# Seven-product quads: T2 subtracted from the weights by an accumulating transfer instead of by VectorE

## The chip, the cores and the metric

The kernel runs on one core of a Trainium2 chip. The metric is the time of one execution on the device in microseconds. Before the change it is 1385.69 us, the median of three runs (1385.48 to 1386.45).

The core has five engines that matter here: TensorE (PE, matrix products into PSUM), VectorE (DVE) and ScalarE (ACT) for elementwise work, GpSimd (POOL), and SyncE (SP), which here only issues transfers (DMAs). Each engine takes its instructions strictly in the order of its own queue and waits at semaphores for the others. Sixteen DMA engines move data between HBM and SBUF.

## The reference

One layer of a hybrid block on x of 256 rows and 2048 columns, in float32: RMS norm, one large projection, a dilated attention branch, a state-space (SSD) branch, gates, and an output projection.

```python
hn = rms_norm(x, norm_w)
proj = hn @ w_in
q, k, v, z_a, z_s, xbc, dt_raw, g_a, g_s = jnp.split(proj, split_points, axis=-1)
# attention of q, k, v in three dilations -> o_a ; scan of xbc, dt_raw -> y
merged = jax.nn.sigmoid(g_a) * (o_a @ w_attn_branch) + jax.nn.sigmoid(g_s) * (y @ w_ssm_branch)
x = x + merged @ w_out
return rms_norm(x, final_norm_w)
```

## The kernel before

All large products are made on TensorE from float32 values split in two: for a weight tile w, ScalarE writes h, a rounded copy, and VectorE writes l = w - h. A product then takes three matmuls (x_h by h, x_h by l, x_l by h; lines 476 to 478, the helper `triple`). The weights (nearly all of the 314.87 MB that are read) are streamed from HBM in units of 128 x 1024 (512 KB) through a ring of five slots (`W_BUFS`), by SP's queue.

Ten wide products use pairs of column blocks and are made by `gemm_pair`: ssm, v, ga, attn and out, each for c = 0 and c = 2. `gemm_pair` goes over the inner dimension in steps of two tiles of 128, called quads, in an order given by a table. A plain quad needs two weight units and 24 matmuls. A quad listed in `S_QUADS` (43 of them) is a Strassen-like step on 2 x 2 blocks: seven products in place of eight, 21 matmuls. Its weight operands are

- `wa`, the unit with the blocks B11 and B21 (loaded, line 522), split into `ha`, `la`;
- `wc`, the block B22 (128 x 512, line 526), split into `hc`, `lc`;
- `wt`, with T1 = B12 - B11 in its left half and T2 = B22 - T1 in its right half, mostly made earlier, kept in HBM (`presum`) and loaded (line 525); for some quads it is made here from a tile `wb` (lines 548 and 555); split into `ht`, `lt` (htt and ltt in the profile);
- `wa` minus T2 on both halves, written over `wa` after `ha` and `la` have read it (line 557), split into `hu`, `lu` (htu and ltu). In part of v, ht, lt, hu and lu lie in a tile `tl_v`.

The helper `part` makes each split: line 543 on ScalarE, line 544 on VectorE; `unit` does it for plain units (lines 276 and 277). Outside v, the tiles of ht and hu have two buffers for both together, so ht of a quad reuses the buffer of the quad before it.

A scheduler in the tile framework sets the order on each engine. The block from line 547 on stands under `tc.high_priority(L_AHEAD)`, which lets a quad's preparation be issued well ahead of its products. GpSimd has little to do in the quads: one-element copies (line 432) on which SP's fetches of the left operands wait.

Of the kernel before, what the change touches and what calls it, by code (L numbers as in the profile page):

```python
# [11 lines left out]
AF = mybir.ActivationFunctionType  # L12
ALU = mybir.AluOpType
PSUM = bass.MemoryType.PSUM

P = 128
# [180 lines left out]
def hybrid_block(ctx: ExitStack, tc: tile.TileContext, wall, xt, x, pk_d, cst_d, fw_d, out):  # L197
    nc = tc.nc
    ve, ac, gp, pe = nc.vector, nc.scalar, nc.gpsimd, nc.tensor
# [24 lines left out]
    def bank(tag, bufs, name):  # L224
        return ps.tile([P, 512], F32, name=name, tag=tag, bufs=bufs)
# [9 lines left out]
    def ring(name):  # L235
        return stream.tile([P, UNIT], F32, name=name, tag="w", bufs=W_BUFS)
# [30 lines left out]
    def unit(n, shape):  # L267
        if n not in loaded:
            load(n)
        w = loaded.pop(n)  # L270
        h = stream.tile([P, UNIT], F32R, name=f"h{n}", tag="h", bufs=H_BUFS)
        l = stream.tile([P, UNIT], F32R, name=f"l{n}", tag="l", bufs=H_BUFS)
        cuts = (0, UNIT // 2, UNIT) if n < N_FINE else (0, UNIT)
        with tc.high_priority(L_AHEAD) if n >= KT // UB else nullcontext():
            for a, b in zip(cuts, cuts[1:]):
                ac.activation(h[:, a:b], w[:, a:b], AF.Copy)  # L276
                ve.tensor_tensor(l[:, a:b], w[:, a:b], h[:, a:b].bitcast(F32), ALU.subtract)  # L277
        for f in on_unit.pop(n, ()):
            f(h[:, 0:1].bitcast(F32))
        k, m = shape  # L280
        return h.rearrange("p (k m) -> p k m", k=k), l.rearrange("p (k m) -> p k m", k=k)
# [34 lines left out]
    def tick(final=False):  # L316
        now[0] += 1
        run_due(float("inf") if final else now[0])
# [142 lines left out]
    def gemm_pair(tag, x_of, n_kt, sxs, swap, extra={}, close=1, order=None, room={}, tail=None):  # L461

        name = f"{tag[0]}{tag[1]}"
        quads = S_QUADS[tag]
        n_q = n_kt // 2
        first = FIRST[tag]
        tags = ("g", "g", "g", "g"), ("m1", "m1", "m2", "m2")
        e_tags, p_tags = tags[::-1] if swap else tags  # L470

        def banks(ts, s):
            return [bank(t, 4 if t == "g" else 2, f"{s}_{name}_{n}") for n, t in enumerate(ts)]

        def triple(acc, xh, xl, h, l, start, stop):
            pe.matmul(acc, xh, h, start=start, stop=False)  # L476
            pe.matmul(acc, xh, l, start=False, stop=False)  # L477
            pe.matmul(acc, xl, h, start=False, stop=stop)  # L478

        es = banks(e_tags, "ps")  # L480
        prods = []
        order = order or range(n_q)
        seven = [q for q in order if q in quads]
        for at, q in enumerate(order):
            tick()
            for f in extra.get(q, ()):
                f()
            ks = [x_of(2 * q + k) for k in range(2)]
            a = [[(x[:, i * P : (i + 1) * P], x[:, S + i * P : S + (i + 1) * P]) for x in ks] for i in range(2)]
            n = first + 2 * q  # L490
            if q not in quads:
                ready = [] if at <= n_q - close else ready
                ready += [(a, k, *unit(n + k, (2, 512))) for k in range(2)]
                if n_q - close <= at < n_q - 1:
                    continue
                steps = [(e, i, c) for e in ready for i in range(2) for c in range(2)]
                if at == n_q - 1:
                    steps.sort(key=lambda s: s[1:])
                jobs = [(e, i, c, es[2 * i + c], WHOLE, at == 0 and e[1] == 0, e is ready[-1]) for e, i, c in steps]
                if tail and at == n_q - 1:  # L500
                    es.append(tail(prods))
                    _, i, c = steps[-1]
                    jobs = jobs[:-3]
                    for acc, cs in ((es[3][:, LEFT], LEFT), (es[4][:, LEFT], RIGHT)):
                        for n, e in enumerate(ready[-3:]):
                            jobs.append((e, i, c, acc, cs, cs is RIGHT and n == 0, n == 2))
                for (ae, k, h, l), i, c, acc, cs, start, stop in jobs:
                    triple(acc, *ae[i][k], h[:, c, cs], l[:, c, cs], start=start, stop=stop and at == n_q - 1)
                continue
            if not prods:  # L510
                prods = banks(p_tags, "pp")
            made = (tag, q) in presum

            def place(kind):
                if not room.get(kind):
                    t = ring(f"{kind}{n}")
                    return t[:, 512:] if kind == "wc" else t
                seats[kind] = seats.get(kind, -1) + 1
                return room[kind][seats[kind] % len(room[kind])]

            wa = ring(f"wa{n}")
            nc.sync.dma_start(wa, wall[n])
            if made:
                wt, wc = place("wt"), place("wc")
                nc.sync.dma_start(wt, presum[tag, q])
                nc.sync.dma_start(wc, wall[n + 1, :, 512:])
            else:
                wt = ring(f"wb{n}")
                wc = wt[:, 512:]
                nc.sync.dma_start(wt, wall[n + 1])  # L530

            def hl(where, suffix, tags, bufs):
                return [
                    where.tile([P, UNIT], F32R, name=f"{t}{suffix}{n}", tag=t, bufs=bufs) for t in tags
                ]

            def pair_of(suffix):
                sets = room.get("tl", ())
                seats["tl"] = (seats.get("tl", -1) + 1) % (2 + len(sets))
                return sets[seats["tl"] - 2] if seats["tl"] > 1 else hl(mul, suffix, ("ht", "lt"), 2)  # L540

            def part(src, h, l):
                ac.activation(h, src, AF.Copy)  # L543
                ve.tensor_tensor(l, src, h.bitcast(F32), ALU.subtract)  # L544

            two = lambda t: t.rearrange("p (k m) -> p k m", k=2)
            with tc.high_priority(L_AHEAD):
                if not made:
                    ve.tensor_tensor(wt[:, :512], wt[:, :512], wa[:, :512], ALU.subtract)
                ha, la = hl(stream, "a", "hl", H_BUFS)  # L550
                part(wa, ha, la)
                hc, lc = hl(stream, "c", "hl", H_BUFS)
                part(wc, hc[:, :512], lc[:, :512])
                if not made:
                    ve.tensor_tensor(wt[:, 512:], wt[:, 512:], wt[:, :512], ALU.subtract)
                t2 = wt[:, 512:].unsqueeze(1).to_broadcast([P, 2, 512])
                ve.tensor_tensor(two(wa), two(wa), t2, ALU.subtract)
                ht, lt = pair_of("t")
                part(wt, ht, lt)
                hu, lu = pair_of("u")  # L560
                part(wa, hu, lu)
            sx = sxs[q]
            lo, hi = slice(0, 512), slice(512, 1024)
            go, end = q == seven[0], q == seven[-1]
            for acc, x, h, l, cs, own in (
                (prods[0], a[0][0], ha, la, lo, True),
                (es[0], a[0][1], ha, la, hi, False),
                (es[1], sx[3], hc, lc, lo, False),
                (prods[1], sx[0], ht, lt, lo, True),
                (prods[2], sx[2], ht, lt, hi, True),  # L570
                (prods[3], sx[1], hu, lu, lo, True),
                (es[2], a[1][1], hu, lu, hi, False),
            ):
                triple(acc, *x, h[:, cs], l[:, cs], start=(own and go), stop=(own and end))
        return es, prods
# [457 lines left out]
    with tc.tile_pool(name="att", bufs=2) as ap:  # L1033
# [75 lines left out]
        for c in (0, 2):  # L1109
            es, prods = gemm_pair(  # L1110
                ("ga", c), lambda kt: XT[:, kt, :], KT, sx_of_x, c == 2, order=G_ORDERS[c], room=room
            )
            open_gate(c, es, prods)
        tick(final=True)

    with tc.tile_pool(name="fin", bufs=2) as fp:
# [58 lines left out]
        for c0 in (0, 2):  # L1175
# [6 lines left out]
            def tail(prods):  # L1182
                add_folded(prods)
                return bank("g", 4, "ps_right")
# [87 lines left out]
```

## Time and profile before

| | |
|---|---|
| median of the runs | 1385.69 us |
| the profiled execution: its span, first to last instruction | 1383.8 us |
| TensorE / VectorE / ScalarE / GpSimd busy | 1373.6 / 1169.5 / 835.5 / 142.0 us |
| HBM read / written | 314.87 / 28.77 MB |
| five stretches with quads (ssm, v, ga, attn, out) | about 600 to 832 and 1115 to 1376 us |

How to read the profile's rows: `L557 DVE TENSOR_TENSOR wa<-wa,wt` is an instruction of line 557 on VectorE that writes wa and reads wa and wt; buffer numbers are left out. After the count (x13) stand the busy time in us, the mean of one in ns, and the idle time of the engine just before them with what ended it. In the view of waits a row says who waited for whom: total us, times, longest. A row of the DMA view ends with the median time from issue to landing. The profile is of one execution.

### The profile page before, as it was taken

Reading aid. Unit: us, or ns where it says so; the run is one execution under the profiler, and the core shown is the slowest. Engines: PE = TensorE matmul, PEld = TensorE weight load, DVE = VectorE, ACT = ScalarE, POOL = GpSimd, SP = SyncE. Lnnn points to the kernel's source line nnn. Section 1 sums busy time; section 2 is a strip of 40 time slices with the busy share of each in tenths; the row PEclk is TensorE's granted clock in tenths of the full one; section 3 lists DMA queues with packets and bytes.
Section 4 is the critical chain, followed back from the end, with each engine's and each line's share of the span. In section 5 each row is a group of like instructions: output and inputs, shape, how many; then the busy total and the mean of one; then the engine's idle time right before and its main releaser. Section 6 shows DMA issues by size and latency. Waiting matters only on the chain.

```text
span 1383.8 us, 20696 instructions
## 1 busy us (share of the span) xinstructions
PE 1373.6 (99%) x7266; PEld 1169.9 (85%) x7266; DVE 1169.5 (85%) x1753; ACT 835.5 (60%) x1306; POOL 142.0 (10%) x226
## 2 busy tenths in 40 slices
PE   9999999999999999999999999999999999999997
PEld 8888888888888888888888888888888888888886
DVE  7898999987799898789889897777877788888897
ACT  7656677675667675766565554544544556655564
POOL 2301111101011100010001001111111000000112
PEclk9999999999999999999999999999999999999999
DMA  9767988868787866668677668888888757865773
GB/s 347 231 187 225 313 254 291 279 224 287 245 266 240 294 212 208 188 224 280 230 259 267 222 209 278 275 275 273 299 288 301 241 161 264 294 222 180 243 273 122
DMA packets 105080, 345.00 MB, mean 249 GB/s; under 512 B 11728, under 2 KB 13712, under 8 KB 104976
## 3 DMA queue, kind: packets, MB, share of 16 engines
q1 hardware_dynamic: 103536, 339.62, 74.0%
q10 hardware_dynamic: 1440, 4.06, 0.8%
q8 instruction: 57, 0.93, 0.3%
q14 instruction: 47, 0.39, 0.1%
HBM read 314.87 MB, written 28.77 MB: 248 GB/s over the span
## 4 chain that ended last, share of the span: by engine, by line
PE 97%; DMA 1%; DVE 1%; ACT 1%; issue 0%; SPq 0%; POOL 0%; POOLq 0%; DVEq 0%; ACTq 0%
PE ps_zs L329 8%; PE ps_xs L329 8%; PE ps_zs L332 4%; PE ps_q L329 4%; PE ps_za L329 4%; PE ps_k L329 4%; PE ps_xs L332 4%; PE ps_ssm L476 3%; PE ps_ssm L477 3%; PE ps_ssm L478 3%; PE ps_q L332 2%; PE ps_k L332 2%; PE ps_za L332 2%; PE ps_gs L414 2%; PE ps_gs L412 2%; PE ps_gs L413 2%
## 5 line engine op out<-in xcount | busy, mean ns | idle before, releaser
L276 ACT ACTIVATE h<-w 128x1024 fp32r<-128x1024 f32 (+1 forms) x398 | 413.9, 1047 | 318.0 <-issue 78.8
L277 DVE TENSOR_TENSOR l<-w,h 128x1024 fp32r<-128x1024 f32 (+1 forms) x398 | 479.4, 1211 | 124.2 <-ACT h L276 121.8
L329 PE MATMUL ps_zs<-XT,h 128*128 128x512 f32 x496 | 176.3, 397 | 0.0
L329 PE MATMUL ps_xs<-XT,h 128*128 128x512 f32 x496 | 175.9, 396 | 0.0
L332 PE MATMUL ps_zs<-XT,l 128*128 128x256 f32 x496 | 139.9, 282 | 0.0
L332 PE MATMUL ps_xs<-XT,l 128*128 128x256 f32 x496 | 139.8, 282 | 0.0
L329 PEld LDWEIGHTS ps_xs<-XT,h 128*128 128x128 f32 x496 | 93.3, 188 | 21.7
L329 PEld LDWEIGHTS ps_zs<-XT,h 128*128 128x128 f32 x496 | 93.4, 188 | 21.2
L332 PEld LDWEIGHTS ps_zs<-XT,l 128*128 128x128 f32 x496 | 93.7, 189 | 1.5 <-issue 0.7
L332 PEld LDWEIGHTS ps_xs<-XT,l 128*128 128x128 f32 x496 | 93.7, 189 | 0.4
L329 PE MATMUL ps_q<-XT,h 128*128 128x512 f32 x256 | 92.5, 405 | 0.2 <-ACT h L276 0.2
L329 PE MATMUL ps_k<-XT,h 128*128 128x512 f32 x256 | 89.9, 395 | 0.0
L329 PE MATMUL ps_za<-XT,h 128*128 128x512 f32 x256 | 89.7, 394 | 0.0
L543 ACT ACTIVATE ha<-wa 128x1024 fp32r<-128x1024 f32 x43 | 45.4, 1055 | 46.4 <-DMA wa<-in_wall 10.9
L332 PE MATMUL ps_q<-XT,l 128*128 128x256 f32 x256 | 71.2, 278 | 0.0
L332 PE MATMUL ps_k<-XT,l 128*128 128x256 f32 x256 | 71.1, 278 | 0.0
L332 PE MATMUL ps_za<-XT,l 128*128 128x256 f32 x256 | 71.1, 278 | 0.0
L544 DVE TENSOR_TENSOR la<-wa,ha 128x1024 fp32r<-128x1024 f32 x43 | 52.5, 1220 | 11.9 <-ACT ha L543 11.8
L782 ACT ACTIVATE gt<-acb,acT 128x128 f32<-128x128 f32 x128 | 44.2, 391 | 23.7 <-DMA acb<-acum_d 21.9
L329 PEld LDWEIGHTS ps_q<-XT,h 128*128 128x128 f32 x256 | 48.2, 188 | 11.5 <-ACT h L276 0.6
L329 PEld LDWEIGHTS ps_za<-XT,h 128*128 128x128 f32 x256 | 48.1, 188 | 11.3
L329 PEld LDWEIGHTS ps_k<-XT,h 128*128 128x128 f32 x256 | 48.1, 188 | 11.2
(688 smaller groups left out, 3325.1 us busy)
## 6 DMA issues: line engine op xcount, KB each, us to landing
w<-in_wall SPq DMA_DIRECT2D x394, 512.0 KB, 4.7
wa<-in_wall SPq DMA_DIRECT2D x43, 512.0 KB, 4.9
th_a<-in_wall SPq DMA_DIRECT2D x19, 512.0 KB, 5.6
sums_at<-in_wall SPq DMA_DIRECT2D x18, 512.0 KB, 4.7
acb<-acum_d SPq DMA_DIRECT2D x32, 256.0 KB, 4.0
t_ssm<-sums_at SPq DMA_DIRECT2D x13, 512.0 KB, 4.1
wt<-t_ssm SPq DMA_DIRECT2D x13, 512.0 KB, 5.4
th_a<-in_wall SPq DMA_DIRECT2D x19, 256.0 KB, 6.0
```

The costliest lines, as they stand in the source:

```text
L276: ac.activation(h[:, a:b], w[:, a:b], AF.Copy)
L277: ve.tensor_tensor(l[:, a:b], w[:, a:b], h[:, a:b].bitcast(F32), ALU.subtract)
L329: pe.matmul(acc, h[:, kk, :], m, start=(kt == 0), stop=False)
L332: pe.matmul(acc[:, S:], l[:, kk, :], m[:, :S], start=False, stop=(kt == KT - 1))
L412: pe.matmul(accs[i], xh, h[:, kk], start=(kt == 0), stop=False)
L413: pe.matmul(accs[i], xh, l[:, kk], start=False, stop=False)
L476: pe.matmul(acc, xh, h, start=start, stop=False)
L477: pe.matmul(acc, xh, l, start=False, stop=False)
L478: pe.matmul(acc, xl, h, start=False, stop=stop)
L543: ac.activation(h, src, AF.Copy)
L544: ve.tensor_tensor(l, src, h.bitcast(F32), ALU.subtract)
L782: ac.activation(g4[:, n, b], acb[:, j, b // 2 * P : b // 2 * P + P], AF.Relu, scale=-1.0, bias=sc[:, h : h + 1],)
```

## The change

For each of the 43 quads the subtraction on VectorE is dropped. In its place, once ht and lt have been made from wt, ScalarE negates T2 in place (128 x 512), and GpSimd issues a transfer from SBUF to SBUF that adds the negated T2 to both halves of wa (128 x 1024). After that wa is split into hu and lu as before.

```diff
                 if not made:
                     ve.tensor_tensor(wt[:, 512:], wt[:, 512:], wt[:, :512], ALU.subtract)
-                t2 = wt[:, 512:].unsqueeze(1).to_broadcast([P, 2, 512])
-                ve.tensor_tensor(two(wa), two(wa), t2, ALU.subtract)
                 ht, lt = pair_of("t")
                 part(wt, ht, lt)
                 hu, lu = pair_of("u")
+                minus = wt[:, 512:]
+                ac.activation(minus, minus, AF.Copy, scale=-1.0)
+                gp.dma_start(two(wa), minus.unsqueeze(1).to_broadcast([P, 2, 512]), accum_op=ALU.add)
                 part(wa, hu, lu)
```

The lines behind it move by one: the negation is line 560 and the transfer line 561. The scheduler orders the engines anew. Below, 239, 241 and 245 are the weight units of the quads 7, 8 and 10 of ssm at c = 2, and h233 and h234 belong to the plain quad 4.

ScalarE, before, from ha of quad 7 to ha of quad 10:

```order
L543 ACTIVATE ha239_7351<-wa239_7346 128x1024
L543 ACTIVATE hc239_7355<-room_s_6440 128x512
L543 ACTIVATE htt239_7360<-wt239_7348 128x1024
L543 ACTIVATE ha241_7394<-wa241_7389 128x1024
L543 ACTIVATE htu239_7364<-wa239_7346 128x1024
L543 ACTIVATE hc241_7398<-room_s_6440 128x512
L276 ACTIVATE h233_7434<-w233_7432 128x1024
L276 ACTIVATE h234_7440<-w234_7438 128x1024
L543 ACTIVATE htt241_7403<-wt241_7391 128x1024
L543 ACTIVATE ha245_7473<-wa245_7468 128x1024
L543 ACTIVATE htu241_7407<-wa241_7389 128x1024
```

ScalarE, now, from htt of quad 7 to htu of quad 8 (line 560 is the negation):

```order
L543 ACTIVATE htt239_7368<-wt239_7357 128x1024
L543 ACTIVATE ha241_7404<-wa241_7399 128x1024
L543 ACTIVATE hc241_7408<-room_s_6440 128x512
L560 ACTIVATE wt239_7357<-wt239_7357 128x512
L276 ACTIVATE h233_7445<-w233_7443 128x1024
L543 ACTIVATE htu239_7372<-wa239_7355 128x1024
L543 ACTIVATE htt241_7412<-wt241_7401 128x1024
L560 ACTIVATE wt241_7401<-wt241_7401 128x512
L276 ACTIVATE h234_7451<-w234_7449 128x1024
L543 ACTIVATE ha245_7484<-wa245_7479 128x1024
L543 ACTIVATE hc245_7488<-room_s_6440 128x512
L543 ACTIVATE htu241_7416<-wa241_7399 128x1024
```

Now htt and the negation of quad 8 stand right behind htu of quad 7, and htu of quad 8 has moved behind ha and hc of quad 10.

VectorE at the same place, before:

```order
L544 TENSOR_TENSOR ltt239_7361<-wt239_7348,htt239_7360 128x1024
L557 TENSOR_TENSOR wa239_7346<-wa239_7346,wt239_7348 128x1024
L544 TENSOR_TENSOR la241_7395<-wa241_7389,ha241_7394 128x1024
L544 TENSOR_TENSOR ltu239_7365<-wa239_7346,htu239_7364 128x1024
L557 TENSOR_TENSOR wa241_7389<-wa241_7389,wt241_7391 128x1024
L544 TENSOR_TENSOR lc241_7399<-room_s_6440,hc241_7398 128x512
L277 TENSOR_TENSOR l233_7435<-w233_7432,h233_7434 128x1024
L277 TENSOR_TENSOR l234_7441<-w234_7438,h234_7440 128x1024
L544 TENSOR_TENSOR ltt241_7404<-wt241_7391,htt241_7403 128x1024
```

VectorE, now:

```order
L544 TENSOR_TENSOR ltt239_7369<-wt239_7357,htt239_7368 128x1024
L544 TENSOR_TENSOR la241_7405<-wa241_7399,ha241_7404 128x1024
L544 TENSOR_TENSOR lc241_7409<-room_s_6440,hc241_7408 128x512
L277 TENSOR_TENSOR l233_7446<-w233_7443,h233_7445 128x1024
L544 TENSOR_TENSOR ltu239_7373<-wa239_7355,htu239_7372 128x1024
L544 TENSOR_TENSOR ltt241_7413<-wt241_7401,htt241_7412 128x1024
```

The two subtractions of line 557 are gone, and ltt of quad 8 stands directly behind ltu of quad 7.

TensorE, before, where the first matmuls with htu of quad 8 stand (pp and ps are the PSUM tiles, yT, sx_y the left operands):

```order
L478 MATMUL pp_ssm2_2_7186<-htt241_7403,sx_y8_6578 128x512
L476 MATMUL ps_ssm2_3_7147<-h234_7440,yTb_82 128x512
L476 MATMUL pp_ssm2_3_7187<-htu241_7407,sx_y8_6578 128x512
L476 MATMUL ps_ssm2_2_7146<-htu241_7407,yT18_4759 128x512
L477 MATMUL ps_ssm2_3_7147<-l234_7441,yTb_82 128x512
L478 MATMUL ps_ssm2_3_7147<-h234_7440,yTb_82 128x512
L476 MATMUL pp_ssm2_0_7184<-ha245_7473,yT18_4759 128x512
```

TensorE, now:

```order
L476 MATMUL pp_ssm2_0_7191<-ha245_7484,yT18_4759 128x512
L476 MATMUL ps_ssm2_0_7151<-ha245_7484,yT18_4759 128x512
L476 MATMUL ps_ssm2_1_7152<-hc245_7488,sx_y10_6676 128x512
L477 MATMUL pp_ssm2_0_7191<-la245_7485,yT18_4759 128x512
L478 MATMUL pp_ssm2_0_7191<-ha245_7484,yT18_4759 128x512
L477 MATMUL ps_ssm2_0_7151<-la245_7485,yT18_4759 128x512
L478 MATMUL ps_ssm2_0_7151<-ha245_7484,yT18_4759 128x512
L477 MATMUL ps_ssm2_1_7152<-lc245_7489,sx_y10_6676 128x512
L478 MATMUL ps_ssm2_1_7152<-hc245_7488,sx_y10_6676 128x512
L476 MATMUL pp_ssm2_3_7194<-htu241_7416,sx_y8_6578 128x512
L476 MATMUL ps_ssm2_2_7153<-htu241_7416,yT18_4759 128x512
L476 MATMUL pp_ssm2_1_7192<-htt245_7492,yT18_4759 128x512
```

The products with htu of quad 8 have moved behind the first nine matmuls of quad 10. They stand 30 matmuls behind the first with htu of quad 7, which begin at the row `pp_ssm2_3_7194<-htu239_7372`.

## The prediction

> **What bounds the kernel now.** I read the page's first and fourth parts, then the waits of TensorE, then the stages in which the quads stand.
>
> ```profile
> span 1383.8 us, 20696 instructions
> PE 1373.6 (99%) x7266; PEld 1169.9 (85%) x7266; DVE 1169.5 (85%) x1753; ACT 835.5 (60%) x1306; POOL 142.0 (10%) x226
> ...
> PE 97%; DMA 1%; DVE 1%; ACT 1%; issue 0%; SPq 0%; POOL 0%; POOLq 0%; DVEq 0%; ACTq 0%
> ```
>
> TensorE is busy for 99% of the span, and 97% of the chain that ended last runs on it. The other engines have idle time. The view of waits, cut to TensorE, is three lines long:
>
> ```profile
> PE warm L623 <- DVE ssq L620: 1.4, 1, 1.4
> PE ps_first L377 <- ACT h L276: 0.3, 1, 0.3
> PE ps_q L329 <- ACT h L276: 0.2, 1, 0.2
> ```
>
> So TensorE waits 1.9 us in the whole program, and none of it in a seven-product quad. The quads lie in five stretches (ssm, v, ga, attn, out). The columns below are busy time with counts, granted clock, share of the DMA engines and GB/s:
>
> ```profile
> 600.00:745.00 145.00, 145.00 (x642) 120.11 (x641) 125.92 (x132) 88.25 (x96) 3.60 (x6) 1.00 0.77 260
> 745.00:832.00 87.00, 86.80 (x387) 71.54 (x386) 78.72 (x86) 46.98 (x53) 3.96 (x4) 1.00 0.65 222
> 1115.00:1210.00 95.00, 95.00 (x435) 79.10 (x434) 82.13 (x102) 58.58 (x75) 3.17 (x4) 1.00 0.74 252
> 1210.00:1300.00 90.00, 90.00 (x407) 74.56 (x406) 79.65 (x94) 49.86 (x59) 3.34 (x2) 1.00 0.63 207
> 1300.00:1376.00 76.00, 75.50 (x350) 62.85 (x348) 68.36 (x84) 42.29 (x60) 11.50 (x12) 1.00 0.60 204
> ```
>
> TensorE has no hole there, VectorE is 87 to 92% busy but always ahead, and the DMA engines are 60 to 77% busy. **A saving on VectorE has nothing to shorten; a delay on the way to TensorE has nowhere to hide but in the lead of the operands.**
>
> **What is removed.** All 43 subtractions of L557, in one row (VectorE busy time, count):
>
> ```profile
> 600.00:1376.00 776.00, 52.48 (x43) 1.00 0.74 248
> ```
>
> 52.5 us leave VectorE. On the path they are worth 0, since TensorE never waited for VectorE in these stretches.
>
> **What is added, per quad.** A ScalarE pass over 128x512, then a GpSimd transfer that reads T2 twice (512 KB), reads wa (512 KB) and writes wa (512 KB). The nearest rows:
>
> ```profile
> L543 ACT ACTIVATE hc<-room_s 128x512 fp32r<-128x512 f32 x13 | 8.0, 616 | 1.0 <-ACT htu L543 1.0
> L543 ACT ACTIVATE htu<-wa 128x1024 fp32r<-128x1024 f32 x38 | 40.0, 1053 | 21.0 <-PE ps_ga L478 6.3 <-DVE wa L557 5.8 <-PE ps_ssm L478 3.6
> L544 DVE TENSOR_TENSOR ltu<-wa,htu 128x1024 fp32r<-128x1024 f32 x38 | 46.4, 1221 | 11.0 <-ACT htu L543 10.9
> L544 DVE TENSOR_TENSOR ltt<-wt,htt 128x1024 fp32r<-128x1024 f32 x13 | 15.8, 1219 | 0.2 <-ACT htt L543 0.2
> ```
>
> The negation costs 0.62 us; 43 of them are 27 us on ScalarE, which is 61% busy in its fullest stretch (88.25 of 145), so as work they are free. As a link they are not: T2 may be negated in place only after htt and ltt have read it, and hu may start only when the transfer has landed. Before, hu hung on one VectorE pass of 1.22 us that needed neither htt nor ltt.
>
> The transfer itself is in no row. The nearest:
>
> ```profile
> GB/s 347 231 187 225 313 254 291 279 224 287 245 266 240 294 212 208 188 224 280 230 259 267 222 209 278 275 275 273 299 288 301 241 161 264 294 222 180 243 273 122
> ...
> wa<-in_wall SPq DMA_DIRECT2D x43, 512.0 KB, 4.9
> ...
> t_ssm<-sums_at SPq DMA_DIRECT2D x13, 512.0 KB, 4.1
> wt<-t_ssm SPq DMA_DIRECT2D x13, 512.0 KB, 5.4
> ...
> room_s<-in_wall SPq DMA_DIRECT2D x13, 256.0 KB, 4.1
> ...
> out<-fin SPq DMA_DIRECT2D x5, 256.0 KB, 2.4
> ```
> ```profile
> L247 POOL COPY sums_at<-h 128x1 f32<-128x1 f32 x36 | 23.3, 679 | 132.0 <-ACT h L276 100.9 <-DMA acb<-acum_d 11.3 <-PE dt_tp L742 10.7
> ```
>
> My value for L, from the negation's end to the landing, has four parts. A plain load of the same size lands in 4.9 us. The second read, 512 KB at the 347 GB/s of the first slice, is 1.5 us. GpSimd needs some 0.68 us for its smallest copy, so I add 0.5 us for its share in issuing (an estimate). For crowding I add 0.8: each transfer moves twice a load's reads, about 3 us of all DMA engines, so fifteen in the first stretch ask for 45 of 145 us, a share of 0.31 on top of 0.77; 256 KB take 4.1 us at that share against 2.4 us at the end of the program, and I take half of those 1.7 us. **L = 7.7 us.** Lower end: the 2.4 us of out<-fin plus 256 KB more, 0.8, gives 3.2 us. Upper end: wt's 5.4 us once for each operand read, 10.8 us. 7.7 is nearer to the loads, which cross the same stretches.
>
> The Trainium skill, page "DMA: Bandwidth & Descriptors", section "Anatomy of one DMA — SWDGE (gpsimd) path", fits a GpSimd-issued transfer as about 2.0 us plus bytes over 436 GB/s, that is 3.2 us here (an estimate from its figures), by which the sum would be the lower end below. No row here is GpSimd-issued; the plain 512 KB loads, at a median of 4.9 us, speak against reading it as the time in a crowded stretch.
>
> **The loop this closes.** ScalarE and VectorE take their work in the order shown above the prediction. There htu of quad 7 stands ahead of htt of quad 8, and ltu ahead of ltt, and both wait for the transfer. So one quad's transfer must land before the next one's can be prepared: transfer lands, htu 1.05, ltu 1.22, next ltt 1.22 (its htt runs beside ltu), negation 0.62, and four handovers of about 0.1:
>
> ```profile
> 605.37 1.04 ACT L543 ACTIVATE htu<-wa 128x1024 fp32r<-128x1024 f32 x1
> ```
> ```profile
> 606.44 1.23 DVE L544 TENSOR_TENSOR ltu<-wa,htu 128x1024 fp32r<-128x1024 f32 x1 [0.26 <-ACT htu L543]
> ```
>
> (htu ends at 606.41, ltu starts at 606.44; 0.1 leaves room.) 1.05 + 1.22 + 1.22 + 0.62 + 0.4 = 4.5 us, so **the period of a quad is P = 4.5 + L = 12.2 us.**
>
> TensorE's side: matmuls start one every (1.07 - 0.39) / 3 = 0.227 us:
>
> ```profile
> 600.99 1.07 PE L476 MATMUL ps_ssm<-h,yTa 128*128 128x512 f32 x4
> ```
>
> In the changed order I counted the matmuls from the first with htu of one quad to the first with htu of the next, for the 40 neighbours within a stretch, and multiplied. From quad 7 to 8 they are 30, so 6.8 us. Sorted: ten from 5.2 to 7.5 us (sum 64.3), six of 8.2, three from 8.9 to 9.5 (27.7), four of 10.2, one of 10.4, five from 11.1 to 11.7 (57.4), then 12.3 three times, 13.4, 13.8, and six from 15.4 to 22.9. Where the distance is under P, TensorE stands for the difference. At P = 12.2 these are the first 29, whose sum is 249.8: 29 x 12.2 - 249.8 = **104 us**. At L = 3.2 (P = 7.7): 10 x 7.7 - 64.3 = 12.7 us. At L = 10.8 (P = 15.3): 34 x 15.3 - 313.9 = 206 us.
>
> I count no recovery in long distances: only two pairs of ht and hu tiles exist outside v, so ScalarE cannot run far ahead. Behind a waiting htu also stand the next ha and the h of plain units; behind a waiting transfer on GpSimd stand the L432 casts that release fetches on SP. I price these at 0, covered by the wait already counted, and the range carries them. On SP no load moves past a new wait except that a slot of wa, held longer, frees later; five slots cover that until L is near the upper end.
>
> The profiled execution spans 1383.8 us, the median of the runs is 1385.69, so 1.9 us lie around the span. 1383.8 + 104 + 1.9 = **1490 us**.
>
> **Rivals.**
> - *The transfer is nearly hidden.* With L of 3.2 to 4.5 us the sum is 13 to 31 us: 1398 to 1416. For it: TensorE waits nowhere now, and the new order itself moves hu's products behind the next quad's ha and hc. Against it: no load or store of 512 KB has a median under t_ssm's 4.1 us, and this one reads twice as much. 0.14.
> - *The transfer is the long kind.* Reading, adding and writing may not overlap, or transfers may queue behind the loads. L of 11 or more gives over 206 us: 1592 and up; at 12 us (P = 16.5) some 250 us, 1636. For it: the DMA share would reach about 1 in the first stretch by my own estimate. 0.13.
> - *Faster: matmuls pace up where VectorE is quieter.* Equal matmuls take
>
> ```profile
> L477 PE MATMUL ps_out<-l,mT 128*128 128x512 f32 (+1 forms) x96 | 37.0, 387 | 0.0
> ...
> L477 PE MATMUL ps_ssm<-l,yTa 128*128 128x512 f32 x56 | 21.9, 392 | 0.0
> ```
>
>   5 ns apart. If that were VectorE's traffic, the 2221 matmuls of the five stretches would gain 11 us: 1375. It decides only if L stays under about 3 us. Against it: the quicker ones stand where VectorE is busier (68.36 of 76 us against 125.92 of 145). 0.03.
> - That VectorE's work stays is excluded: in the built order its 43 rows are gone.
>
> **How the numbers follow.** Forecast (the loop binds, L between 4.5 and 11) 0.66, long transfer 0.13, nearly hidden 0.14, no visible change 0.04, faster 0.03. Under 0.2%, 2.8 us, a measurement of this kernel cannot tell a change from none. Faster 0.03, same 0.04, slower 0.93. The range runs from 1405 (part of the hidden case) to 1625 (L of about 11.7): it leaves out about 0.1 below and 0.09 above.
>
> **What would show it.** Right: TensorE's waits gain rows on htu and tl_v of L543, some 100 us in all; ScalarE's wait before htu is on the transfer into wa; the group of negations takes 0.62 us; transfers land in 6 to 9 us; the ssm stretch grows most. Granted clock below 1.00 in a quad stretch would be a cost I left out. Wrong: landing times near 3 us with TensorE still 99% busy (hidden), or waits on h of plain units larger than those on htu (then loads and slots bind, not the loop).

## The result and the profile after

The changed kernel takes **1549.88 us** (median of 4 runs, 1546.43 to 1552.27) against 1386.07 us for the kernel before on the same chip (1385.48 to 1386.52): a ratio of 1.1182, 95% interval 1.1166 to 1.1197. That is 163.8 us lost. The prediction was 1490 us, range 1405 to 1625: the sign and the place were right, L came out somewhat longer than predicted, and 60 of the 164 us were missing.

The page of the changed kernel, its first part and the row of the granted clock (one digit for each of 40 slices, 9 for 90% or more):

```profile
span 1550.5 us, 20832 instructions
PE 1436.8 (93%) x7266; PEld 1191.7 (77%) x7266; DVE 1127.2 (73%) x1710; ACT 860.7 (56%) x1349; POOL 188.6 (12%) x269
...
PEclk9999999999999999989999989999999999889998
```

TensorE's idle time rose from 10.2 us (1383.8 - 1373.6) to 113.7 us (1550.5 - 1436.8), that is by 103.5, and its busy time by 63.2 us, for the same 7266 matmuls: where the clock's digit is 8, some of them ran at half clock (a granted clock of 0.50). VectorE lost its 42 us and has nothing to show for it.

The waits of TensorE, then of ScalarE (total, times, longest, in us):

```profile
PE pp_ssm L476 <- ACT htu L543: 24.7, 10, 6.3
PE pp_v L476 <- ACT tl_v L543: 10.7, 4, 5.6
PE pp_ga L476 <- ACT htu L543: 10.3, 3, 6.2
PE pp_attn L476 <- ACT htu L543: 6.8, 3, 3.6
...
PE ps_ssm L476 <- ACT h L276: 6.5, 5, 1.9
```
```profile
ACT htu L543 <- DMA wa<-wt: 47.9, 13, 7.5
...
ACT htu L543 <- DMA wa<-th_a: 30.7, 7, 9.0
...
ACT h L276 <- DMA w<-in_wall: 29.2, 26, 3.7
...
ACT htu L543 <- DMA wa<-fin: 25.5, 6, 7.4
```

Before, TensorE waited 1.9 us in all. Now it waits for hu (64 us in all its rows on htu and tl_v of L543), ScalarE waits for the transfer, and the rows of the second view in which an added transfer into wa ends the wait add up to 167.4 us in 41 waits, of which one, 9.8 us of fin, is not for hu. Waits for plain loads (29.2 us, 11.3 before) are small beside that.

The groups of the added instructions, and the DMA view (its last number is the median from issue to landing):

```profile
L560 ACT ACTIVATE wt<-wt 128x512 f32<-128x512 f32 x13 | 8.1, 624 | 4.2 <-DVE ltt L544 4.1
```
```profile
L561 POOL DMA_DIRECT2D wa<-wt x13 | 16.0, 1228 | 140.0 <-ACT wt L560 106.1 <-DVE lc L544 23.0 <-DMA room_v<-in_wall 9.6
```
```profile
wa<-in_wall SPq DMA_DIRECT2D x43, 512.0 KB, 4.7
...
wa<-wt POOLq DMA_DIRECT2D x13, 512.0 KB, 6.3
...
wa<-wb POOLq DMA_DIRECT2D x6, 512.0 KB, 7.5
...
wa<-room_o POOLq DMA_DIRECT2D x4, 512.0 KB, 5.4
```

Over all 43, issue to landing is 6.9 us in the median (7.3 in the mean, 4.8 to 10.6), and in 33 of them the issue starts some 0.4 us behind the negation's end; ten start later, up to 26 us, four of these when la has been made from wa. From the negation's end to the landing, which is what L means, it is 8.4 us in the median and 9.5 in the mean, predicted 7.7. The Trainium skill's fit for a GpSimd-issued transfer (page "DMA: Bandwidth & Descriptors", section "Anatomy of one DMA — SWDGE (gpsimd) path"), which gave 3.2 us, does not hold in this stretch, nor for the plain copies of e6 (5.15 us); the measurement decides.

One quad in the timeline of ScalarE (start, duration, instruction, idle before it and what ended it), and TensorE at its beginning:

```profile
728.22 1.06 ACT L543 ACTIVATE htu<-wa 128x1024 fp32r<-128x1024 f32 x1 [7.51 <-DMA wa<-wt]
729.18 1.04 ACT L543 ACTIVATE htt<-wt 128x1024 fp32r<-128x1024 f32 x1
...
731.70 0.63 ACT L560 ACTIVATE wt<-wt 128x512 f32<-128x512 f32 x1
734.52 1.06 ACT L276 ACTIVATE h<-w 128x1024 fp32r<-128x1024 f32 x1 [2.19 <-PE ps_ssm L478]
739.05 1.06 ACT L543 ACTIVATE htu<-wa 128x1024 fp32r<-128x1024 f32 x1 [3.47 <-DMA wa<-wt]
```
```profile
729.33 0.80 PE L476 MATMUL pp_ssm<-htu,sx_y 128*128 128x512 f32 x1 [4.83 <-ACT htu L543]
...
731.29 0.63 PE L477 MATMUL pp_ssm<-ltu,sx_y 128*128 128x512 f32 x1
731.72 0.63 PE L478 MATMUL pp_ssm<-htu,sx_y 128*128 128x512 f32 x1
```

There are htu, htt, ha and hc of the next quad (left out above), the negation, one plain h, a dead stretch until the landing, and htu again: 10.8 us from one htu to the next. TensorE takes htu 0.05 us after it is made (729.28 to 729.33). Its matmuls soon start 0.43 us apart (731.29 to 731.72), not 0.227: half clock. The loop itself is there: in 10 of the 42 pairs of transfers in a row the next issue starts 4.55 to 4.62 us behind a landing. That is some 4.1 us to the negation's end, where 4.5 were predicted, and 0.4 to the issue.

### The profile page after: what moved, and what is told of

It reads as the page before. It is cut to its first block, busy times and chain, and to the rows that moved or that the text cites. A ratio compares the mean times of both kernels' runs of the same rounds, so it can differ in the third digit from the quotient of the medians.

```text
span 1550.5 us, 20832 instructions
## 1 busy us (share of the span) xinstructions
PE 1436.8 (93%) x7266; PEld 1191.7 (77%) x7266; DVE 1127.2 (73%) x1710; ACT 860.7 (56%) x1349; POOL 188.6 (12%) x269
## 5 line engine op out<-in xcount | busy, mean ns | idle before, releaser
L544 DVE TENSOR_TENSOR ltu<-wa,htu 128x1024 fp32r<-128x1024 f32 x38 | 46.6, 1225 | 131.2 <-ACT htu L543 131.2
L543 ACT ACTIVATE htu<-wa 128x1024 fp32r<-128x1024 f32 x38 | 40.2, 1058 | 143.0 <-DMA wa<-wt 47.9
L329 PEld LDWEIGHTS ps_xs<-XT,h 128*128 128x128 f32 x496 | 93.2, 188 | 21.7
L543 ACT ACTIVATE ha<-wa 128x1024 fp32r<-128x1024 f32 x43 | 45.3, 1053 | 33.2 <-PE ps_v L478 12.5
```

Of the source, the lines that this page charges most:

```text
L329: pe.matmul(acc, h[:, kk, :], m, start=(kt == 0), stop=False)
```

## The experiments

The theory at this point: the loop of the prediction, P = 4.5 + L, costs what TensorE stands, and the clock, which falls after each stall, adds the rest. The rivals: traffic of the 43 transfers, the changed order by itself, ring slots held too long, and a cost that every transfer has, however far apart they are. Each time lost below is against runs of the kernel before on the same chip. The scheduler orders each version anew, so that most runs differ from the change in their order too; by the traces e6 alone has the order of the change, on all engines.

| run | what | median us | time lost, us | ScalarE's waits on the added transfers, us |
|---|---|---|---|---|
| | the change | 1549.88 | 163.8 | 167.4 |
| e1 | VectorE adds, no transfer | 1394.98 | 9.1 | 0 |
| e2 | before, plus a transfer nobody reads | 1518.77 | 132.9 | 6.0 |
| e3 | negation ahead of the split of wt | 1481.37 | 95.5 | 128.1 |
| e4 | extra matmuls in the waits | 1557.07 | 171.2 | 194.9 |
| e5 | every second quad | 1450.45 | 65.1 | 69.3 |
| e6 | copy, not add | 1478.51 | 93.1 | 91.1 |
| e7 | before, with e4's matmuls | 1445.50 | 60.1 | 0 |
| e8 | before, plus tiny transfers | 1412.01 | 26.6 | 6.6 |
| e9 | before, 7 ring slots, 3 of h and l | 1409.70 | 24.0 | 0 |
| e10 | the change, the same | 1554.99 | 169.3 (145.3 over e9) | 153.4 |
| e11 | the change, hu and lu on GpSimd | 1559.75 | 174.0 (101.2 over e12) | 10.1 |
| e12 | before, hu and lu on GpSimd | 1458.54 | 72.8 | 0 |

(In e2, e8 and e11 the last column is the one wait of fin.)

### e1: the addition on VectorE

```diff
-                gp.dma_start(two(wa), minus.unsqueeze(1).to_broadcast([P, 2, 512]), accum_op=ALU.add)
+                ve.tensor_tensor(two(wa), two(wa), minus.unsqueeze(1).to_broadcast([P, 2, 512]), ALU.add)
```

> The negation stays on ScalarE and the new order of dependencies stays, but VectorE adds the negated T2 (1.22 us and one handover of 0.1 us) in place of the transfer. Loop theory: the period of a quad is 4.5 + 1.3 = 5.8 us; of the 40 distances only those from 5.2 to 5.8 us lie under it, so TensorE waits 0 to 6 us, the granted clock stays at 1.00, and the time is 1386 to 1395 us. If the new link (negation behind htt and ltt, hu behind both) or the changed order costs by itself, whatever does the addition: at least 1440 us.

Measured 1394.98 us, ratio 1.0067 (1.0052 to 1.0083), TensorE busy for 1377.0 of 1393.1 us. The negation and the dependence on htt and ltt together cost 9 us, in an order of their own: of the 42 distances in matmuls from one quad's hu to the next, only 12 are within 3 of those in the change. So e1 clears these two, but not the change's order; e6, in exactly that order, bears on it (below).

### e2 and e8: a transfer for which no engine waits

```diff
                 hu, lu = pair_of("u")
                 part(wa, hu, lu)
+                gp.dma_start(two(wa), t2, accum_op=ALU.add)
```

> The kernel before, VectorE's subtraction kept, plus the same accumulating transfer of T2 onto wa after hu and lu have been made from it: its result is used by nothing. Same bytes, same issues on GpSimd, a slot of wa is held as long, but nothing waits for the landing except the next load into that slot. Loop theory: 1386 to 1400 us. Traffic theory (43 transfers slow the loads, or the slots come free too late): at least 1450 us, with TensorE waiting for h of plain units. If the loads crowd the transfers, these land in 6 to 8 us here too; if not, in 3 to 5 us.

Measured 1518.77 us, ratio 1.0943 (1.0903 to 1.0983). The loop theory was wrong here by over 100 us. In the views of waits of e2, ScalarE and SyncE:

```profile
ACT h L276 <- DMA w<-in_wall: 121.4, 55, 7.6
```
```profile
SPq L265 <- DMA wa<-fin: 33.4, 4, 10.1
...
SPq L522 <- DMA wa<-th_a: 27.7, 3, 9.3
...
SPq L265 <- DMA wa<-wt: 26.9, 7, 5.5
```

SyncE issues the loads in order. A load into a slot (or a place of wt) that a transfer still uses stands for up to some 10 us, and every load behind it too; then ScalarE waits for plain weights, 121.4 us against 11.3 before. The transfers also come one at a time: none is issued before the one ahead has landed, and 15 of 42 start 0.3 us behind that landing. From the end of ltu to the landing it is 10.3 us in the median. In e8 the side transfer moves two columns only:

```diff
+                gp.dma_start(wa[:, :2], wt[:, 512:514], accum_op=ALU.add)
```

> As e2, but the side transfer adds two columns of T2 (1 KB in all) to two columns of wa: the same wait of GpSimd for ltu, the same issue, the slot of wa is held until it lands, but no traffic to speak of. If e2's 133 us came from traffic: 1386 to 1395 us. If they came from the slot held past ltu and from GpSimd's and SP's ordered queues standing behind it: the time goes with the landing, a landing of 2 to 4 us in place of 9 gives 1415 to 1460 us.

Measured 1412.01 us, ratio 1.0192 (1.0172 to 1.0213). It lands after 3.5 us in the median in place of 9.3 in e2, and 27 of 133 us remain, with ScalarE's wait for plain weights at 53.3 us. That rules out a fixed cost of 43 issues on GpSimd of the size of e2's loss. It doesn't part bytes from holding time: both shrank.

### e3: the negation ahead of the split of wt

```diff
+                minus = wt[:, 512:]
+                ac.activation(minus, minus, AF.Copy, scale=-1.0)
+                gp.dma_start(two(wa), minus.unsqueeze(1).to_broadcast([P, 2, 512]), accum_op=ALU.add)
                 ht, lt = pair_of("t")
                 part(wt, ht, lt)
                 hu, lu = pair_of("u")
-                minus = wt[:, 512:]
-                ac.activation(minus, minus, AF.Copy, scale=-1.0)
-                gp.dma_start(two(wa), minus.unsqueeze(1).to_broadcast([P, 2, 512]), accum_op=ALU.add)
...
-        ve.tensor_tensor(d12, p6, d11, ALU.add)
+        ve.tensor_tensor(d12, d11, p6, ALU.subtract)
```

> As the changed kernel, but T2 is negated, and the transfer issued, before ht and lt are made from wt; ht then holds the negative of T2 and line 582 subtracts that product instead of adding it, so the result is the same. In the built order the negation of quad 8 now stands ahead of htu of quad 7, so two transfers can be under way at once; that of quad 10 still stands behind htu of quad 8. Loop theory: half of the periods shrink to nothing, the others are L + 1.05 + 0.62 + 0.3 = 9.3 us against longer distances: TensorE waits 5 to 35 us, up to 20 us more by the clock: 1391 to 1440 us. If each transfer costs a fixed time wherever it stands: 1540 to 1560 us.

Measured 1481.37 us, ratio 1.0692 (1.0676 to 1.0708): neither. The trace shows that what the run was to bring about did not happen: no transfer was issued before the one ahead had landed. Twelve of 42 issues start 0.3 us behind that landing, and others wait for la, which has to read wa first. The waits of GpSimd in e3:

```profile
POOL wa L558 <- DVE la L544: 132.9, 13, 26.2
```

So e3 says that a link without htt and ltt (in another order) costs 69 us less. It is no test of two transfers under way at once, and its 95 us do not speak against the rule of distances.

### e4 and e7: extra matmuls in the waits

```diff
+FILL = {207: 1, 209: 6, 215: 2, 219: 7, 235: 5, 247: 2, 249: 1, 251: 2, 261: 2, 267: 2, 281: 6, 283: 3, 285: 2, 389: 2, 395: 2, 397: 7, 425: 4, 429: 1, 437: 2, 443: 2, 455: 5}
...
+                if h is hu and own:
+                    for _ in range(FILL.get(n, 0)):
+                        pe.matmul(es[2], sel, lt[:, lo].bitcast(F32), start=False, stop=False)
                 triple(acc, *x, h[:, cs], l[:, cs], start=(own and go), stop=(own and end))
...
+        ac.activation(sel, sel, AF.Copy, scale=0.0)
```

> The changed kernel with 64 matmuls more, of a zero stationary tile (the dead 128x128 tile sel, zeroed) by lt, added to a bank that is open anyway, placed ahead of the products with hu in the 21 quads before whose hu products TensorE waited: 1 to 7 in each, as many as fill the wait at an estimated 4 x 0.227 = 0.91 us each (they are plain float32 matmuls), 58 us in all. If the clock that drops after the waits adds to the time (63 us), and the loop sets only the 100 us of waiting: the clock stays at 1.00 and the time falls to 1490 to 1515 us. If the loop on ScalarE and VectorE sets the time, and matmuls at half clock only fill time in which TensorE would wait for hu anyway: 1540 to 1560 us, with the clock at 1.00 in most of the stretches. If TensorE is what sets the time there: about 1608 us.

> Control to e4: the same 64 extra matmuls in the kernel before, where TensorE does not wait. They cost what they last, 58 us by the estimate: 1435 to 1450 us. If it is much less, e4 says nothing on filled waits.

(The table makes 66 matmuls, not 64.) In the kernel before they cost 60.1 us, ratio 1.0434 (1.0413 to 1.0455), 0.91 us each. In the changed kernel they cost 7.2 us: 1557.07 against 1549.88. The first part of e4's page:

```profile
span 1554.9 us, 21119 instructions
PE 1472.6 (95%) x7398; PEld 1206.9 (78%) x7398; DVE 1126.1 (72%) x1710; ACT 860.3 (55%) x1350; POOL 186.9 (12%) x269
```

TensorE does 57 us more work (its busy time grew by that in e7), yet is busy only 35.8 us longer and idle 31.4 us less: the stretches at half clock in the quads fell from 102 to 61 us, and the time did not fall with them. Against e7, with the same matmuls, TensorE is busy 41.6 us longer, where it was 63.2 for the change: some 22 us of slow matmuls are gone. So **that part of the half clock added next to nothing**. The reading is that slow matmuls fill time in which TensorE would wait for hu, and that the chain through ScalarE and the transfer sets the time. For the 61 us that stay at half clock this is not tested, and e4's order is another than the change's.

### e5: every second quad

```diff
+                if seven.index(q) % 2:
+                    minus = wt[:, 512:]
+                    ac.activation(minus, minus, AF.Copy, scale=-1.0)
+                    gp.dma_start(two(wa), minus.unsqueeze(1).to_broadcast([P, 2, 512]), accum_op=ALU.add)
+                else:
+                    t2 = wt[:, 512:].unsqueeze(1).to_broadcast([P, 2, 512])
+                    ve.tensor_tensor(two(wa), two(wa), t2, ALU.subtract)
```

> The change in every second seven-product quad of a product only (20 of 43); the others keep VectorE's subtraction. Loop theory of the prediction (a quad's transfer must land before the next quad can be prepared, and only distances under 12.2 us cost anything): between two transfers now lie two distances, of which hardly any sum is under 12.2 us plus the preparation of the quad between; 1386 to 1410 us. Dead-time theory (each transfer stops ScalarE for the part of L that its order does not fill, about 4 us, and the few tiles of h, l, ht and hu do not let it make that up, however long the distance): 20 of 43 of the 164 us, that is 76 us, 1450 to 1475 us.

Measured 1450.45 us, ratio 1.0479 (1.0457 to 1.0501): 3.3 us for each of 20 transfers, against 3.8 for each of 43. By the distances there was hardly anything to lose. For example, from the first matmul with hu of quad 5 of ssm at c = 2 to that of quad 8, the next with a transfer, there are 79 matmuls, 17.9 us, far above P; it took 21.7 us. Within the products no two transfers in a row are less than 13.4 us of matmuls apart. This is the run that fells the rule of distances.

### e6: copy in place of add

```diff
-                gp.dma_start(two(wa), minus.unsqueeze(1).to_broadcast([P, 2, 512]), accum_op=ALU.add)
+                gp.dma_start(two(wa), minus.unsqueeze(1).to_broadcast([P, 2, 512]))
```

> The changed kernel with the transfer overwriting wa by the negated T2 instead of adding to it (hu and lu are then made from minus T2, so the output is another): T2 is read twice and wa written once as before, but wa is not read and nothing is added. If adding is a good part of the landing time (6.9 us median), it lands in 4 to 5.5 us, the waits of ScalarE before htu fall by about 2 us in each of 43, and the time falls by 43 x 2 = 86 us at most: 1460 to 1500 us. If the landing is GpSimd's issue and the crowd of loads: 1535 to 1555 us.

Measured 1478.51 us, ratio 1.0671 (1.0655 to 1.0687). Its transfers in the DMA view:

```profile
wa<-wt POOLq DMA_DIRECT2D x13, 512.0 KB, 5.1
...
wa<-th_a POOLq DMA_DIRECT2D x8, 512.0 KB, 5.1
```

This version leaves the addition out. The median over all is 5.15 us against 6.9: reading wa and adding are 1.75 us of the landing, and 0.5 of them are GpSimd's own instruction, which takes 0.72 us in place of 1.21. Shortening each L by 1.75 us gains 71 us, 1.66 us each: nearly all of L's end is on the path. As every engine's order is that of the change, this is the cleanest run of all: the order by itself can't be what these 71 us come from.

### e9 and e10: more ring slots

```diff
-W_BUFS, H_BUFS = 5, 4
+W_BUFS, H_BUFS = 7, 3
```

> Control to e10: the kernel before with seven ring slots in place of five and three tiles of h and of l in place of four (the same SBUF). More loads ahead, one pair of split weights less ahead: 1386 to 1430 us; no theory of the change speaks of it.

> The changed kernel with seven ring slots and three tiles of h and l. Slot theory (what makes each transfer cost its dead time is that wa holds a slot for some 10 us longer, so that the loads come late): SyncE's waits on transfers into wa fall from 196 us to under 60, and the difference to e9 falls from 164 us to under 80. Theory of ScalarE standing still before htu: its waits on the transfers stay at 130 us or more, and the difference to e9 stays at 130 to 200 us.

The kernel before takes 1409.70 us with these (ratio 1.0174, 1.0144 to 1.0203), the change 1554.99 (1.1222, 1.1173 to 1.1271): 145.3 us apart. ScalarE in e10:

```profile
ACT htu L543 <- DMA wa<-th_a: 32.6, 7, 8.7
ACT htu L543 <- DMA wa<-wt: 30.8, 11, 8.1
...
ACT h L276 <- DMA w<-in_wall: 7.6, 7, 1.8
```

With seven slots ScalarE hardly waits for plain weights any more (7.6 us), and nearly the whole loss stays. In the change as it stands, the ring is not what binds. SyncE's waits on transfers stayed at 196 us: half of them stand at loads of wt (L525), and the other half at loads into the ring, 98 us against 92 in the change. Two more slots did not shorten these either, but hardly anything behind them waited.

### e11 and e12: hu and lu on GpSimd

```diff
-                part(wa, hu, lu)
+                gp.tensor_copy(hu, wa)
+                gp.tensor_tensor(lu, wa, hu.bitcast(F32), ALU.subtract)
```

> Control to e11: the kernel before with hu and lu made on GpSimd. Two passes over 128x1024 on GpSimd take perhaps 2 to 5 us in place of 2.3 us; if TensorE's lead covers that: 1386 to 1400 us, else up to 1480 us.

> The changed kernel with hu and lu made on GpSimd, which does little else there, instead of on ScalarE and VectorE: the transfer takes as long, but ScalarE and VectorE never wait for it. If all of the cost is that these two stand still in their order: against e12 the difference falls from 164 us to under 50. If the lateness of hu itself, or the slot of wa held until it lands, costs as much (as in e2, where nothing but the slot waited and 133 us were lost): 100 us or more against e12, with ScalarE now waiting for loads or for TensorE to free tiles.

e12 takes 1458.54 us (1.0526, 1.0485 to 1.0568), e11 1559.75 (1.1257, 1.1222 to 1.1291): 101.2 us apart. The waits of GpSimd and of ScalarE in e11:

```profile
POOL htu L562 <- DMA wa<-wt: 66.7, 11, 8.7
```
```profile
ACT h L276 <- DMA w<-in_wall: 82.3, 34, 6.6
```

ScalarE and VectorE no longer stand at the transfer, and 101 of 164 us remain. So their standing in order is a part of the cost at most, about 63 us by this pair; hu itself is still late, and ScalarE now waits for plain weights (82.3 us, 35.6 in e12). The pair is no clean one, for GpSimd's own passes (1.3 and 2.7 us in e11) are slower and stand in its order too.

## Why the prediction was right, and where it was short

*That VectorE's saving is worth nothing*: right. VectorE fell by 42 us of busy time, and no wait of TensorE before could use it.

*That the transfer is the cost, not the negation*: right; e1 keeps the negation and its place behind htt and ltt and loses 9 us. That the changed order is not the cost is shown by e6 for 71 us; no run has that order without a transfer.

*L = 7.7 us*: close, 8.4 in the median (9.5 in the mean). The parts were less sure than the sum: e6 gives 1.75 us for reading wa and adding, GpSimd's instruction is 1.2 us long where I had allowed 0.5 for its share, and that an issue may also have to wait for la was no part of it.

*Where it shows*: right. TensorE waits for htu and tl_v of L543, ScalarE for the transfer into wa, and waits for plain h are small. The ssm stretch grew most, by 64 us. The rows add up to 64 us, not the "some 100 us" I named; matmuls at half clock filling the waits would account for that.

*The granted clock*: I wrote that a clock below 1.00 in a quad stretch would be a cost left out. It fell, and TensorE was busy 63 us longer; e4 speaks against adding this to the sum, for the 22 us of it that e4 took away. That idle time alone grew by 103.5 us, where 104 were predicted, is a coincidence.

*The step that failed* is "Where the distance is under P, TensorE stands for the difference", with "I count no recovery in long distances" meant as a small correction. From the trace of the change, the 29 neighbours under 12.2 us lost 115 us against their matmuls, 104 predicted: the period was sized well (12.6 us in the mean). But the 11 longer ones, predicted to lose nothing, lost 30 us, 2.7 each, and the rest, about 20 us, lies outside these 40 pairs (5.6 us from attn to out, 4.2 ahead of the first quad). e5 shows it without mixture: at twice the distance a transfer costs nearly the same.

What the rule left out is how far hu is made ahead of its use. In the kernel before (htu ends at 605.37 + 1.04 = 606.41 by the row in the prediction), TensorE:

```profile
609.83 0.39 PE L476 MATMUL pp_ssm<-htu,sx_y 128*128 128x512 f32 x1
```

That is a lead of 3.4 us. Over the 43 quads the trace gives 2.9 us in the mean, and the same in long distances (3.1) as in short ones (2.9): a long distance gives no longer lead. In the change it is 0.05 us in the median. The link grew by the negation 0.62, the issue 0.41 and the landing 6.9 us, less the 1.22 us of the dropped VectorE pass: 6.7 us. Less the lead, 2.9, each quad is 3.8 us late; times 43 is 163 us, and 163.8 were measured. That it comes so near is luck: 6.9 is a median, and with the mean landing of 7.26 the sum is 179. With medians it gives for e5 (landing 6.54, 20 quads) 69 us, measured 65.1; for e6 (landing 5.15) 89, measured 93.1. For e10 (landing 6.55, a lead of 2.1 in e9) it gives 185, measured 145.3, and for e3 (landing 7.30) 181, measured 95.5, or 83 if the 2.3 us of htt and ltt are taken off the link. This account was made after the runs; no run tested it afresh, and it is argued, not shown.

What stays open is what keeps the lead at some 3 us in the kernel before. Ring slots alone do not (e10), ScalarE's order alone does not (e11). The two pairs of ht and hu and the four tiles of h and l were not varied upwards; e9, with three of h and l, has a shorter lead. And e2 suggests that the slots, SyncE's order and transfers that come one at a time would be the next bound close behind: 133 us with nobody waiting for the result.

None of the versions beats the kernel before, whose TensorE already is 99% busy.

## What to carry to other kernels

Compare a link that gets longer with the lead of its result over its use, taken from the trace for each place, before anything else: here 2.9 us of lead against 6.7 us of added link, times the number of places, gives the size of the loss in the change, e5 and e6, though not in e10. Distance between the places helped little: at twice the distance (e5) a transfer cost 3.3 us in place of 3.8. And before adding up idle time and slow clock as two costs, fill the idle time with work and see whether the time follows the clock.

## What the runs showed of the hardware

**The clock falls after much less than a full idle window.** In the trace of the change the clock changes on a fixed grid of 3.41 us (the half-clock stretches last 3.41 or 6.83 us within the quads). The view by windows, cut on that grid (TensorE's busy time is the second number, its granted clock the third from the end):

```profile
660.54:663.95 3.41, 1.66 (x7) 0.75 (x5) 1.39 (x2) 1.32 (x2) 0.00 (x0) 1.00 0.81 225
663.95:667.36 3.41, 2.57 (x6) 2.09 (x7) 2.70 (x3) 2.69 (x3) 0.00 (x0) 0.50 0.70 247
762.94:766.35 3.41, 1.84 (x8) 1.54 (x9) 1.61 (x2) 2.95 (x4) 0.96 (x1) 1.00 0.37 144
766.35:769.76 3.41, 3.41 (x16) 2.51 (x14) 2.74 (x4) 0.20 (x1) 0.25 (x1) 1.00 0.90 192
```

With 1.75 us idle of 3.41 the next window ran at half clock; with 1.57 us it did not. Over all windows at full clock in this trace, up to 1.6 us idle kept it, from 1.95 us on it always fell, and between the two both happened. (In e9 it fell once after 1.44 us.) The Trainium skill, page "TensorE: Matmul & The Clock Gate", section "HAM oscillation — how this bites in real kernels", asks for no idle gaps over about 3.4 us; here about half of that in one window was enough.

**An accumulating transfer inside SBUF is slow to land, and a tiny one is not quick**: 6.9 us for 512 KB added, 5.15 us copied (e6), 3.5 us for 1 KB added (e8), all beside a busy queue of loads.

**The adding transfers came one at a time.** In none of the eight runs with them was one issued from GpSimd before the one ahead had landed. Fifteen of 42 in e2 and twelve of 42 in e3 were issued 0.3 us behind that landing, and the semaphore of that landing is not among those for which their instructions wait. Of the plain copies of e6, one was issued 2.1 us before the landing of the one ahead. What holds them apart is not shown.
